# Ten projection steps moved from ahead of the pointwise products to the first attention scores, with counting budgets and four small copies rearranged

## Chip, cores and metric

One core of a Trainium2 chip runs the whole program. The metric is the device time of one execution in microseconds (us), as the median of several runs. The engines are TensorE (PE, matmuls and transposes), VectorE (DVE), ScalarE (ACT) and GpSimd (POOL); SyncE (SP) and ACT issue the transfers (DMA).

## What is computed

A two-layer decoder trunk over 1104 rows: 1040 rows of a prompt (16 learned tokens and 1024 new ones) and 64 rows of eight running sequences. In each layer three mixers work on the same normalised input, and their gated sum goes through an output projection and is added to the input:

```python
(aq, af, ai, az, b_glu, bz, cq, ck, cv, cqi, cki, cw, cz, gate) = project(h, norm_g, w_in, b_in)
oa, s_new = hgrn_prompt(qa, ka, va, logf)                 # gated linear recurrence
ya = (rmsnorm(oa, gn_g) * silu(az)) @ w_pa
y  = silu(layernorm(depthwise_conv(a * sigmoid(g)) + conv_b))
yb = ((y @ conv_pw) * silu(z)) @ w_pb                     # the pointwise products: y @ conv_pw
sc = index_scores(qi, wi, ki)                             # indexer: every query scores every key
idx, valid = select_keys(sc, causal, 256)                 # the 256 best keys of each query
yc = (sparse_attend(rope(q), rope(k), v, idx) * silu(cz)) @ w_pc
h  = h + (ga * ya + gb * yb + gc * yc) @ w_out
```

## The kernel before

Activations stand with channels on the 128 partitions and rows along the free dimension, in three groups of 384, 384 and 336 columns. Each float32 product is made of three matmuls of a split input (`XH`, `XL`: high part and rest) and a split weight (`wh`, `wl`).

**The stream and its fills.** The 60 blocks of 128 output channels of the input projection, and behind them blocks that start the merge, come from one generator, `stream` (L346). A block is 24 steps: three groups of eight, a step is three matmuls. When a group is complete, ACT moves it out of the bank with its bias (`act_`, recorded as L206). Blocks of cz are moved out twice, as they are and through a sigmoid, and POOL multiplies the two (L408); after the third group the block is stored (L411, DMA `czD<-sp`). These tiles come from a pool of two buffers (`spl`, L170). At a block's first step the weights of the block after it are fetched: one load on SP's queue, two ACT copies (`wh`, L271) and two POOL differences (`wl`, L272). PE's order is the order of the program: `fill(key)` puts `FILL[key]` steps of the stream where it is called. In layer 0, added up from the table, the fill "c0" begins at step 1084 of the stream, the fill "aq" ends at step 1246, and the blocks of cz begin at steps 1152, 1176, 1200 and 1224.

**Counting.** The 256 best keys are found by DVE: it counts, bit by bit, how many scores lie over a threshold (L1009), and then builds seven masks, for 1104 columns and then 384 to 1024, from a comparison, an equality, a scan, a second comparison and a combination each (`topk_masks`, L1020). DVE's order is the program's here too; `masks(key)` puts operations there until their nominal ns, columns + 200, use up `SIDE[key]`, and carries the rest as a debt.

**The stretch of the change.** `conv_out` (L1662) runs, in each layer: DVE's difference for the first group, the fill "c0", `masks("c0")`, and then for each of the three groups four products of twelve matmuls on PE (`dense1`, in three banks, `tp`), each multiplied by DVE with the gate (L1693) and stored, with `masks("cc")` behind each; then the next group's difference (L1676), whose gate POOL multiplies (L1678), `masks("c1")` and the fill "c1". `rope_q` (L727) then rotates the queries: loads of R and X, three DVE operations, and stores. `attention` (L1044) loads keys (`kr`) and values (`vr`), transposes the keys on PE (L1063), splits them on ACT and DVE (L1067 to L1070), loads the queries of the last 128 rows, splits them (`Q`, L1088), runs the fill "aq" and makes the first scores (L1107). In these parts ACT, POOL and SP run an order that a planner makes, not the order of the text.

**The tail queries** are part of the indexer: ACT copies four heads of 16 queries into `qt8` (L857), DVE subtracts the copy from the source (L858). DVE's order holds the convolution's 31 taps between (L1594).

Of the kernel before, what the change touches and what calls it, by code (L numbers as in the profile page):

```python
# [11 lines left out]
def _quiet(msg, *args, **kwargs):  # L12
# [33 lines left out]

FILL = {"n0": 10, "n1": 3, "n2": 0, "s0": 7, "s1": 0, "s2": 3, "ic": 35, "ik": (0, 3, 7), "iq": 7, "is": (6, 4, 7, 6, 7, 7),
# [4 lines left out]
SIDE = {"t0": (5000, 10000, 10000, 10000, 9300, 10000), "tr": (2400, 2400, 2400, 2400, 2400, 2400, 2400, 600, 0),  # L52
# [3 lines left out]
KSEL = 4  # L56
KEEP = 24
EDGE = {mybir.EngineType.DVE, mybir.EngineType.Activation}
# [98 lines left out]
def trunk(tc, a, o, depth=DEPTH):  # L157
# [4 lines left out]
    def f(x):  # L162
        return x.bitcast(F32)
# [41 lines left out]
    def act_(out, in_, fn, **kw):  # L205
        S.activation(out, in_, fn, **kw)  # L206
# [76 lines left out]
    def dense1(w, K, xh, xl, nn, slot=None, between=()):  # L283
        wh, wl = w
        ps = (slot or mmt)()
        ops = [(wh(k), x(k)) for k in range(K) for x in (xh, xl)] + [(wl(k), xh(k)) for k in range(K)]
        between = iter(between)
        for n, (wk, x) in enumerate(ops):
            T.matmul(ps[:, 0:nn], wk, x, start=(n == 0), stop=(n == 3 * K - 1))  # L289
            if n % 6 == 5:  # L290
                next(between, None)
        return ps[:, 0:nn]

    def cols_of(t, n0, nn, k0=0):
        return lambda k: t[:, k0 + k, n0:n0 + nn]
# [140 lines left out]
    class Counting:  # L436
# [23 lines left out]
        def rest(self):  # L460
            while self.high is not None:
                self.ahead()
# [136 lines left out]
    def layer(l, hst, late):  # L599
# [46 lines left out]
        SC8 = scp.tile([128, NT], F32, name="SC8", tag="SC8")  # L646
        fill("ic")
        indexer(l, CTr, SC, SC8, fill, taps, act)
        ctr.close()
        tk1 = tks.enter_context(tc.tile_pool(name="tk1", bufs=1))  # L650
# [19 lines left out]
        with tc.tile_pool(name="tk2", bufs=1) as tk2:  # L670
            masks = Side(itertools.chain(side.gen, topk_masks(SC, SC8, MB, MB8, F, tk2)))
            conv_out(l, pv, pw, late_groups, fill, masks)
            rope_q()
            masks.flush()
# [84 lines left out]
    def indexer(l, CTr, SC, SC8, fill, taps, act):  # L759
        with tc.tile_pool(name="ixc", bufs=1) as xc, tc.tile_pool(name="ixt", bufs=2) as xt:  # L760
# [63 lines left out]
            for i in range(7, 1, -1):  # L824
# [3 lines left out]
                for h in range(4):  # L828
                    ps = lgt()
                    for c0 in range(0, n, 512):  # L830
                        c1 = min(n, c0 + 512)
# [23 lines left out]
            for h in range(4):  # L855
                j, e = divmod(h, 2)
                S.copy(qt8[0:64, h, :], (lo8 if e == 0 else hi8)[:, j, 0:16])  # L857
                V.tensor_tensor(qt8[64:128, h, :], (lo8 if e == 0 else hi8)[:, j, 0:16], f(qt8[0:64, h, :]), op=OP.subtract)  # L858
            CH = ((0, 512), (512, 1024), (1024, NT))

# [15 lines left out]
            for g in range(2):  # L876
                ps = lgt()
                for b in (0, 2):
# [9 lines left out]
                    for n in range(2):  # L888
                        for e in range(2):
                            r, c0 = slice(64 * e, 64 * e + 64), 512 * (n ^ e)  # L890
# [771 lines left out]
    def conv_out(l, pv, pw, groups, fill, masks):  # L1662

        with tc.tile_pool(name="cv2", bufs=2) as c2:
            def load(g):
                n0, nn = groups[g]
                sl = slice(n0, n0 + nn)
                yg, bz, BH, BL = (c2.tile([128, 4, 384], dt, name=nm, tag=nm, bufs=bf)[:, :, 0:nn]
                                  for nm, dt, bf in (("yg", F32, 1), ("bzt", F32, 2), ("BH", F32R, 2), ("BL", F32R, 1)))
                Y.dma_start(yg, yD[:, :, sl].rearrange("c p n -> p c n"))  # L1670
                Y.dma_start(bz, fD["bz"][:, :, sl].rearrange("c p n -> p c n"))
                for c in range(4):
                    S.copy(BH[:, c], yg[:, c])

                def rest():
                    V.tensor_tensor(BL, yg, f(BH), op=OP.subtract)  # L1676
                    act_(yg, bz, AF.Sigmoid)
                    G.tensor_tensor(bz, bz, yg, op=OP.mult)  # L1678
                    return bz, BH, BL

                return rest

            nxt = load(0)()
            fill.upto(32)
            fill("c0")
            masks("c0")
            for g, (n0, nn) in enumerate(groups):
                bz, BH, BL = nxt
                if g < 2:
                    rest = load(g + 1)  # L1690
                for c in range(4):
                    ps = dense1(pw[c], 4, cols_of(BH, 0, nn), cols_of(BL, 0, nn), nn, tpt)
                    V.tensor_tensor(bz[:, c], ps, bz[:, c], op=OP.mult)  # L1693
                    Y.dma_start(obD[c, :, n0:n0 + nn], bz[:, c])
                    masks("cc")
                if g < 2:
                    nxt = rest()
                masks("c1")
                fill("c1", g)


# [173 lines left out]
```

## Time and profile before

| | us |
|---|---|
| median of 3 runs | 2865.78 |
| lowest and highest | 2864.01, 2873.34 |
| the profiled execution, its own time | 2876.56 |
| its span, first to last instruction | 2874.7 |
| PE busy in the span | 2741.0 (95%) |
| DVE, ACT, POOL busy | 2022.6, 1357.9, 1252.4 |
| mean granted clock of PE | 0.985 |

An engine's busy time is an average over stages with different limits. Times in the rows count from the span's first instruction. A wait is put down to what ended last before it. A granted clock of 1.00 is 2.4 GHz, of 0.50 1.2 GHz.

### The profile page before, as it was taken

How to read it: one execution, taken by the hardware profiler on the slowest of the kernel's cores; microseconds unless marked ns; L12 is line 12 of the kernel's file. 1: busy time of each engine (PE TensorE's matmuls, PEld its weight loads, DVE VectorE, ACT ScalarE, POOL GpSimd, SP SyncE). 2: the span in 40 equal slices, each digit the busy share in tenths (PEclk: the TensorE clock that was granted, in tenths of full speed). 3: DMA queues.
4: the chain of work that ended last, by engine and by line, in shares of the span. 5: the costliest groups of instructions: out<-in, count | busy, mean ns of one | idle time of the engine just before them, and what ended most of it. 6: DMA issues, size and time to landing. Idle time of an engine off the chain costs nothing. (4 is left out here: it accounts for less than half of the span.)

```text
span 2874.7 us, 45280 instructions
## 1 busy us (share of the span) xinstructions
PE 2741.0 (95%) x17094; PEld 2607.7 (91%) x17094; DVE 2022.6 (70%) x3518; ACT 1357.9 (47%) x2913; POOL 1252.4 (44%) x1012
## 2 busy tenths in 40 slices
PE   7999989999998999999999999999999989999898
PEld 7999878999998998879999997899999989988798
DVE  5789966878986667545258699688888866774543
ACT  4324546773333556544342345577533245665432
POOL 3544344434424115756464352444444331168453
PEclk9999999999999999999999999999999999999999
DMA  4423233332344224665553232413331442257554
GB/s 149 158 83 113 91 123 121 120 120 98 107 155 150 76 68 151 211 199 175 161 166 108 81 102 99 166 68 117 130 131 62 160 152 76 84 157 234 180 155 151
DMA packets 192570, 374.16 MB, mean 130 GB/s; under 512 B 30656, under 2 KB 129696, under 8 KB 192288
## 3 DMA queue, kind: packets, MB, share of 16 engines
q1 hardware_dynamic: 161856, 270.11, 29.9%
q10 hardware_dynamic: 24608, 80.19, 7.1%
q0 software_dynamic: 5888, 20.97, 2.3%
q8 instruction: 134, 2.20, 0.3%
q14 instruction: 84, 0.69, 0.1%
HBM read 251.07 MB, written 122.40 MB: 130 GB/s over the span
## 5 line engine op out<-in xcount | busy, mean ns | idle before, releaser
L396 PE MATMUL mm<-xh,wh 128*128 128x384 f32 (+2 forms) x2656 | 889.5, 337 | 36.5 <-ACT sp L206 33.0
L396 PE MATMUL mm<-xl,wh 128*128 128x384 f32 (+2 forms) x2656 | 884.9, 336 | 0.0
L272 POOL TENSOR_TENSOR wl<-wr,wh 128x512 fp32r<-128x512 f32 x332 | 483.9, 1474 | 748.4 <-ACT wh L271 468.2
L396 PEld LDWEIGHTS mm<-xh,wh 128*128 128x128 f32 x2656 | 506.3, 191 | 50.8 <-ACT sp L206 40.2
L396 PE MATMUL mm<-xh,wl 128*128 128x384 f32 (+2 forms) x2656 | 525.3, 333 | 0.0
L396 PEld LDWEIGHTS mm<-xl,wh 128*128 128x128 f32 x2656 | 506.3, 191 | 6.9 <-issue 1.4
L396 PEld LDWEIGHTS mm<-xh,wl 128*128 128x128 f32 x2656 | 455.3, 190 | 6.2 <-issue 1.4
L206 ACT ACTIVATE sp<-mm,vec 128x384 f32<-128x384 f32 (+1 forms) x356 | 198.4, 564 | 386.4 <-PE mm L396 371.4
L1009 DVE TENSOR_SCALAR_CACHE_REDUCE jk<-SC,F 128x1024 uint8<-128x1024 f32 (+6 forms) x320 | 334.2, 1044 | 7.8
L1594 DVE SCALAR_TENSOR_TENSOR cy<-up,vec,cy 128x1040 f32<-128x1040 f32 x240 | 336.9, 1404 | 0.5
L271 ACT CAST wh<-wr 128x512 fp32r<-128x512 f32 x352 | 204.3, 617 | 116.3 <-PE mm L396 42.1
L206 ACT ACTIVATE P<-P,nm 128x896 f32<-128x896 f32 (+7 forms) x128 | 99.5, 778 | 72.8 <-DVE nm L1114 70.9
L1130 DVE TENSOR_TENSOR pl<-tp,ph 128x512 fp32r<-128x512 f32 x144 | 97.6, 686 | 36.1 <-ACT ph L1129 35.3
L1595 DVE SCALAR_TENSOR_TENSOR cy<-us,vec,cy 128x64 f32<-128x64 f32 x240 | 118.4, 493 | 0.0
L206 ACT ACTIVATE ja<-SC,hB,hz 80x1104 int8<-80x1104 int16 (+1 forms) x120 | 111.4, 929 | 0.2 <-issue 0.2
L1129 ACT CAST ph<-tp 128x512 fp32r<-128x512 f32 x144 | 83.2, 584 | 54.6 <-PE tp L1126 50.1
L1114 DVE CUSTOM_DVE_ANT_0 P<-sc,MB 128x512 f32<-128x512 f32 (+1 forms) x96 | 63.9, 667 | 55.2 <-PE sc L1108 54.2
L1118 DVE TENSOR_SCALAR P<-P,nm 128x896 f32<-128x896 f32 (+7 forms) x128 | 88.9, 695 | 4.2
L1126 PE MATMUL tp<-ident,P 128*128 128x128 f32 x576 | 87.5, 274 | 1.5 <-DVE P L1118 1.5
L206 ACT ACTIVATE rl<-lg 128x1024 f32<-128x1024 f32 (+6 forms) x54 | 42.6, 789 | 88.9 <-DVE SC L842 35.6
L1107 PE MATMUL sc<-KD,Q 128*128 128x512 f32 (+2 forms) x208 | 71.0, 344 | 11.8 <-DVE Q L1088 7.9
L289 PE MATMUL tp<-xh,wh 128*128 128x384 f32 (+2 forms) x240 | 80.3, 337 | 0.4 <-DVE z L1780 0.4
(472 smaller groups left out, 6072.5 us busy)
## 6 DMA issues: line engine op xcount, KB each, us to landing
wr<-in_wp SPq DMA_DIRECT2D x180, 512.0 KB
eg<-gateD SPq DMA_DIRECT2D x80, 184.0 KB
gateD<-sp ACTq DMA_DIRECT2D x24, 552.0 KB
gateD<-sp ACTq DMA_DIRECT2D x24, 544.0 KB
cr<-in_wc SPq DMA_DIRECT2D x16, 290.0 KB
gt<-gateD SPq DMA_DIRECT2D x24, 192.0 KB
za<-zaD SPq DMA_DIRECT2D x24, 192.0 KB
ggD<-sp ACTq DMA_DIRECT2D x8, 552.0 KB
```

The lines of the kernel that those rows point to most:

```text
L206: S.activation(out, in_, fn, **kw)
L271: S.copy(wh[:, k:k + 4], wr[:, k:k + 4])
L272: (eng or G).tensor_tensor(wl[:, k:k + 4], wr[:, k:k + 4], f(wh[:, k:k + 4]), op=OP.subtract)
L289: T.matmul(ps[:, 0:nn], wk, x, start=(n == 0), stop=(n == 3 * K - 1))
L396: T.matmul(ps, w, x, start=(j == 0), stop=(j == 23))
L1009: V.tensor_scalar(jk[0:rows, 0:n], s, F.bitcast(F32)[0:rows, j:j + 1], None, op0=OP.is_ge, op1=OP.add, accum_out=cnt[0:rows, j:j + 1])
L1118: V.tensor_scalar(p[:, 0:n], p[:, 0:n], nm[:, 3:4], None, op0=OP.mult)
L1126: T.transpose(ps[:, 128 * c:128 * c + 128], P[c][:, 128 * kt:128 * kt + 128], ident)
L1129: S.copy(ph, ps)
L1130: V.tensor_tensor(pl, ps, f(ph), op=OP.subtract)
L1594: V.scalar_tensor_tensor(yp, up[:, j:j + 1040], w, yp, op0=OP.mult, op1=OP.add)
L1595: V.scalar_tensor_tensor(ys, us[:, :, j:j + 8], w, ys, op0=OP.mult, op1=OP.add)
```

## The change

The fill "c0" takes 49 steps instead of 59 and the fill "aq" 26 instead of 16. The counting budget ahead of the first product is 14000 instead of 12000, behind each product 1500 instead of 1200, and behind the three groups 2500, 4500 and 6000 instead of 6000 each. The four copies of the tail queries are written ahead of the four differences.

```diff
-        "hl": (5, 6, 5, 5, 9, 6, 16), "hk": 2, "hs": (0, 1, 0, 1, 0, 1, 0, 4), "ho": 2, "ht": 10, "c0": 59,
-        "c1": (13, 22, 52), "aq": 16, "av": (2, 2, 2, 2, 2, 1, 3, 2), "a0": 6, "as": (3, 1, 1, 1, 2, 1, 0, 1),
+        "hl": (5, 6, 5, 5, 9, 6, 16), "hk": 2, "hs": (0, 1, 0, 1, 0, 1, 0, 4), "ho": 2, "ht": 10, "c0": 49,
+        "c1": (13, 22, 52), "aq": 26, "av": (2, 2, 2, 2, 2, 1, 3, 2), "a0": 6, "as": (3, 1, 1, 1, 2, 1, 0, 1),
...
-        "hs": 1000, "hk": 4000, "ho": 500, "ht": 2000, "he": 5500, "c0": 12000, "cc": 1200, "c1": 6000}
+        "hs": 1000, "hk": 4000, "ho": 500, "ht": 2000, "he": 5500, "c0": 14000, "cc": 1500, "c1": (2500, 4500, 6000)}
...
             for h in range(4):
                 j, e = divmod(h, 2)
                 S.copy(qt8[0:64, h, :], (lo8 if e == 0 else hi8)[:, j, 0:16])
+            for h in range(4):
+                j, e = divmod(h, 2)
                 V.tensor_tensor(qt8[64:128, h, :], (lo8 if e == 0 else hi8)[:, j, 0:16], f(qt8[0:64, h, :]), op=OP.subtract)
...
-                masks("c1")
+                masks("c1", g)
                 fill("c1", g)
```

## Rows read from the trace of the kernel before

**Rows 1.** Waits of PE, 800 to 935 us: us in total, times, longest.

```profile
PE sc L1107 <- DVE Q L1088: 3.9, 1, 3.9
PE tp L289 <- DVE bzt L1693: 2.6, 1, 2.6
PE mm L396 <- ACT sp L206: 2.2, 2, 1.9
PE tp L1063 <- DMA kr<-kvD: 1.2, 1, 1.2
```

**Rows 2.** The same waits of PE over the whole span, both layers.

```profile
PE sc L1107 <- DVE Q L1088: 7.9, 2, 3.9
...
PE tp L289 <- DVE bzt L1693: 5.6, 2, 3.0
```

**Rows 3.** Timeline of DVE, layer 0: start, us, operation, in brackets idle before.

```profile
839.29 0.78 DVE L1034 TENSOR_SCALAR eq<-SC,F 80x1104 bf16<-80x1104 f32 x1
...
842.36 0.56 DVE L1693 TENSOR_TENSOR bzt<-tp,bzt 128x384 f32<-128x384 f32 x1 [2.28 <-PE tp L289]
...
842.83 2.44 DVE L1036 TENSOR_TENSOR_SCAN cs<-eq 80x1104 f32<-80x1104 bf16 x1
...
845.64 1.35 DVE L1038 SCALAR_TENSOR_TENSOR eq<-cs,need,eq 80x1104 bf16<-80x1104 f32 x1
...
889.28 0.50 DVE L1693 TENSOR_TENSOR bzt<-tp,bzt 128x336 f32<-128x336 f32 x1
...
902.83 1.31 DVE L740 TENSOR_TENSOR R<-R,C 128x1104 f32<-128x1104 f32 x1 [6.84 <-DMA X<-rD]
```

**Rows 4.** The timeline of PE, layer 0, from the products to the transposes.

```profile
840.01 0.33 PE L289 MATMUL tp<-BH,ph 128*128 128x384 f32 x1
...
886.12 0.33 PE L396 MATMUL mm<-xh,wh 128*128 128x384 f32 x1
...
907.61 0.42 PE L396 MATMUL mm<-xh,wh 128*128 128x336 f32 x1 [1.88 <-ACT sp L206]
...
907.87 0.32 PE L396 MATMUL mm<-xl,wh 128*128 128x336 f32 x1
...
915.96 1.06 PE L1063 MATMUL tp<-ident,kr 128*128 128x128 f32 x8 [1.25 <-DMA kr<-kvD]
```

**Rows 5.** The timeline of ACT with its DMA issues, layer 0.

```profile
910.14 0.38 ACTq L1056 DMA_DIRECT2D kr<-kvD  x1
...
915.14 0.34 ACTq L411 DMA_DIRECT2D czD<-sp  x1
...
921.99 0.58 ACT L206 ACTIVATE sp<-mm,vec 128x384 f32<-128x384 f32 x1 [1.87 <-DMA czD<-sp]
...
922.60 0.58 ACT L1067 CAST KD<-tp 64x512 fp32r<-64x512 f32 x1
```

**Rows 6.** Windows: stretch, length, busy time by engine, granted clock, DMA share, GB/s.

```profile
809.30:840.00 30.70, 30.70 (x179) 30.22 (x178) 25.79 (x54) 10.83 (x20) 9.27 (x5) 1.00 0.67 225
...
864.90:868.30 3.40, 3.40 (x13) 3.39 (x12) 3.36 (x5) 0.00 (x0) 0.00 (x0) 0.51 0.26 90
...
930.20:933.40 3.20, 3.20 (x12) 2.92 (x11) 1.52 (x5) 1.03 (x1) 0.04 (x1) 0.53 0.32 84
```

**Rows 7.** The timeline of DVE, layer 0, two operations drawn out.

```profile
855.85 2.75 DVE L1034 TENSOR_SCALAR eq<-SC,F 128x512 bf16<-128x512 f32 x1
...
880.93 1.58 DVE L1034 TENSOR_SCALAR eq<-SC,F 128x896 bf16<-128x896 f32 x1
```

**Rows 8.** The timeline of POOL, the product beside the first of them.

```profile
854.50 3.83 POOL L1678 TENSOR_TENSOR bzt<-bzt,yg 128x1536 f32<-128x1536 f32 x1
```

**Rows 9.** The timeline of ACT, layer 0, at the tail queries' copies.

```profile
315.01 0.17 ACT L857 CAST qt<-tp 64x16 fp32r<-64x16 f32 x1 [5.87 <-DVE qt L858]
```

**Rows 10.** The timeline of PE behind those copies, layers 0 and 1.

```profile
316.65 0.42 PE L396 MATMUL mm<-xh,wh 128*128 128x336 f32 x1 [1.23 <-ACT sp L206]
...
1739.10 0.43 PE L396 MATMUL mm<-xh,wh 128*128 128x336 f32 x1 [1.23 <-ACT sp L206]
```

## The prediction

> **What bounds the kernel now.** I read the list of waits of TensorE (PE) first, in the stretch that the change touches: from the pointwise products to the attention's first scores, 800 to 935 us in layer 0. PE waits 9.9 us there, of which 3.9 for the scaled queries Q, 2.6 for a pointwise product's VectorE (DVE) step, 2.2 for ScalarE (ACT) and 1.2 for the keys kr [rows 1]; the list over the whole span adds layer 1, with the same Q wait and a product wait of 3.0 [rows 2]. PE runs an order written out by hand, so all PE work before the first scores plus all its waits gives the time of the first scores; what matters is which chain ends last there.
>
> Then DVE's timeline. DVE counts until 840.07, sits idle 2.28 us, multiplies the first product at 842.36, and from then on is never idle until the last product (889.28 + 0.50) [rows 3]. From that product a chain of transfers runs through the rotation of the queries (X lands for 902.83 [rows 3]) to kr, whose landing frees PE at 915.96 [rows 4]; ACT issues the load of kr at 910.14, after the rotation [rows 3, 5]. I infer that kr's tile lies in memory that the rotation gives back, and take kr to follow the last product at a fixed 26.2 us. Layer 1 I take to repeat all this, as its two waits do [rows 2]. From kr to the first scores at 929.60 (925.68 + 3.92) [rows 1, 4], ACT and DVE split keys and queries, and ACT stands 1.87 us behind the store of a gated block (czD) ahead of the third key copy [rows 5].
>
> **The change part by part.**
>
> *Ten steps leave the fill ahead of the products.* The 59 steps there take 30.70 us [rows 6], 0.52 each, so the products begin 5.2 us earlier, at 834.8 instead of 840.01 [rows 4]. The same ten come back in the fill behind the key transposes, so PE's work before the first scores is unchanged; only its waits can change. With the stream as counted from the fill table, the products begin at step 1133 instead of 1143. The weights of the second cz block (a load on SP's queue, two ACT copies, two GpSimd differences) move from the first fill between products to the second, those of the third block from the second to the last, those of the block after the four from the last fill to behind the query load. The last is the only one that passes a queue's urgent work: its load stands behind the query load, and its copies have at least the 10 steps that were brought there (5.2 us) as cover; without it each us of delay would be a PE wait.
>
> *Counting is spread.* I count the debts by hand. The budget of 14000 adds two operations ahead of the first product, the scan of 2.44 us and the comparison of 1.35 [rows 3]; the later budgets give them back. Up to the last product exactly the same operations stand before as after. So DVE comes to the first product at 840.07 + 2.4 + 1.3 = 843.8. PE has three banks for products: it does three by 834.8 + 6.3 = 841.1 and then waits for DVE to free one at 844.3. **That is a new wait of 3.2 us**, larger than the 2.6 that it had at the second group [rows 1]. In exchange DVE's idle 2.28 us is gone. A wait that long costs more: after the 2.6 us wait the granted clock was 0.51 (the 1.2 GHz level) for 3.4 us [rows 6], which is 1.65 us of PE time. It moves from the second group to the first, where the products that follow wait for DVE anyway.
>
> DVE thus reaches the last product 2.3 us earlier, plus or minus its collisions. An eq of 512 columns took 2.75 us, where one of 1104 columns took 0.78 [rows 3, 7]; it ended 0.3 us after GpSimd's product of 3.83 us [rows 7, 8]. Six operations are drawn out so, from that eq to the eq of 896 columns that took 1.58 [rows 7]; against their pace by columns elsewhere they lose about 8.3 us together, and I put 0.3 less after: 2.6 earlier, bounds 0 and 5. The Trainium skill ("SBUF — State Buffer", Who interferes with whom) says that a two-input DVE operation and a GpSimd operation exclude each other for a whole instruction. By that rule the second group's first product cannot begin before the GpSimd product that follows its difference, near 859.4; if they overlapped it would begin near 856. The trace agrees with the rule, which speaks against moving counting out of the stretches without such products.
>
> *Arrival at kr.* kr lands at 915.96 - 2.6 = 913.4; I take 913.5, because the first cz block's store now meets the rotation's loads. PE leaves the last product at about 882.6 (886.1 before [rows 4]), and 52 steps with a store wait of 1.9 as before (907.61 [rows 4]) bring it to 911 to 912. It waits some 1.5 us for kr; that wait is the slack that hides a store wait of up to 1.4 us at the preceding block boundary, which the dense products hid before.
>
> *From kr to the scores.* Before: 929.60 - 3.92 - 915.96 = 9.7, less a 0.3 wait for ACT, is 9.4 us of PE work. After it is 9.4 + 5.2 = 14.6. Now a boundary between two cz blocks lies four steps into this fill instead of six steps before the transposes. The next block's first evacuation needs the finished block's store. Before, the store issued at 915.14 released ACT at 921.99, 6.85 us later [rows 5]. After: transposes 1.1 [rows 4], four steps, evacuation, GpSimd product and store put the release at 925 to 928.5, while PE runs out of banks at 913.5 + 1.1 + 20 x 0.52 = 925.0. **Wait 0 to 3; I take 1.6**, the middle, since both the store's time and ACT's order are open. First scores: 913.5 + 14.6 + 1.6 = 929.7, against 929.60: +0.1. Q would be ready by 927.1 if its chain kept its 13.6 us, so its 3.9 us wait goes and PE's own work is what comes last.
>
> What is gained is the clock. After the 3.92 us wait the clock was 0.53 from 930.2 to 933.4 with PE busy throughout [rows 6], again 1.65 us. A wait of 1.6 leaves it up (the 1.88 at 907.61 was followed by a matmul of 0.32 us, the usual length [rows 4]). So -1.65.
>
> *The tail queries' copies.* Now ACT's second copy waits 5.87 us for the first difference on DVE, which stands behind convolution taps [rows 9]; behind it on ACT stand evacuations, and PE waits 1.23 us for one in each layer [rows 10]. With all four copies first, ACT never waits for DVE here. The three copies (0.17 each [rows 9]) now delay one earlier evacuation by about 0.4 us, which PE feels in layer 0. Worth 0.8 to 1.2 per layer; bounds 0 and 1.3, taken 0.9.
>
> **Sum.** +0.1 - 1.65 - 0.9 = -2.4 per layer, -4.8 in both. The profiled execution took 2876.56 us (span 2874.7), above the three timed runs and 10.8 over their median of 2865.78. The difference is applied to both: 2871.8 in a profile like it, 2861.0 as a median.
>
> **The rivals.**
> *The wait only moves (no change).* The store wait in the last fill reaches 2.8 instead of 1.6 and the clock falls there: +1.2 and +1.65 per layer against -2.4, about 0, so 2866. For it: the store took 6.85 us [rows 5] and ACT has key copies to do at that moment. Against: the DMA queues are emptier once kr and vr have landed.
> *DVE collides less (faster).* The last product comes 5 us earlier, kr at 911; PE is then limited by its own fill, arrives at 911.5, and with a store wait of 0.5 scores start at 926.6: -3.0 - 1.65 - 0.9 = -5.5 per layer, 2854.8. For it: 8.3 us of collisions are there to be avoided. Against: GpSimd's products follow the same differences in both orders.
> *ACT's queue holds the key copies (slower).* ACT takes the first evacuation behind the store ahead of the third key copy, as it does now at 921.99 and 922.60 [rows 5]. Now this costs 1.87 us; after it the store would release ACT at 927.1, the copy would start at 927.7, and the 7.0 us that separate copy and first scores now (922.60 to 929.60) give 934.7: +5.1 per layer, the clock falls as before, with -0.9 for the copies +4.2, in all +8.4: 2874.2. It decides when the evacuation stands ahead of that copy. Against: the block's first group is now ready 4.2 us later, well after the copy's own inputs.
> *The copies do not do what is said.* If something else holds them, the 0.9 falls away: 2862.8, inside the forecast's own range.
>
> **How the numbers follow.** Forecast 0.50 (own range 2857 to 2864), no change 0.23, faster 0.17, slower 0.10. The faster and the slower case are each cut at about half, leaving 0.16 outside 2854 to 2871. A measurement of this kernel can tell some 0.3%, 8.6 us, from no change, so faster means under 2857.2 (the faster case and the forecast's edge: 0.21), slower over 2874.4 (half of the slower case and a little: 0.06), same 0.73.
>
> **What would show it.** Right: no DVE idle ahead of the first product; a PE wait near 3.2 us at the first group's fourth product with the clock at half behind it, and none over 1 us at the second group; kr 2 to 3 us earlier, counted from the end of DVE's first counting; no wait for Q, and the clock at 1.00 over the first scores; ACT's four tail copies in a row and no 1.23 us wait of PE behind them. Wrong: a Q wait that stays, a store wait over 2.6 us in the last fill, or a last product less than 1 us earlier.

## The result and the profile after

| | before | after |
|---|---|---|
| median of 4 runs each, us | 2866.25 | 2895.57 |
| lowest and highest, us | 2864.01, 2873.34 | 2888.44, 2896.82 |
| the profiled execution, its span, us | 2876.56, 2874.7 | 2888.44, 2886.5 |
| mean granted clock of PE | 0.985 | 0.986 |
| first difference to first scores, layer 0, us | 107.25 | 120.02 |
| the same, layer 1, us | 106.03 | 121.15 |

The ratio is 1.0081, with a 95% interval of 1.0063 to 1.0099: 18 to 28 us slower, where 5 us faster was forecast. The last two lines of the table measure the stretch of the change, from DVE's difference for the first group of products to PE's first scores (822.35 to 929.60 us before, 814.74 to 934.76 after). It grew by 12.8 and 15.1 us, together 27.9 of the 29.3 us between the two medians. Outside the two stretches the profiled execution took 2661 us before and 2645 after, and between 2642 and 2665 in the kernels run below, so the stretch, and not the span, is compared.

PE's waits after the change, 800 to 960 us (us in total, times, longest), to be held against [rows 1]:

```profile
PE mm L396 <- ACT sp L206: 14.8, 4, 8.0
PE tp L289 <- DVE bzt L1695: 2.9, 1, 2.9
PE sc L1109 <- DVE Q L1090: 2.2, 1, 2.2
...
```

The same in layer 1, 2235 to 2380 us:

```profile
PE mm L396 <- ACT sp L206: 15.9, 4, 8.4
PE tp L289 <- DVE bzt L1695: 3.4, 1, 3.4
...
```

One line has grown, PE's wait for a bank that ACT has not moved out: 2.2 us before, 14.8 after. (Behind line 857 the line numbers of after are two higher: L1693 became L1695.) PE's timeline of after shows where; the number in brackets is the idle time before the instruction. It answers to [rows 4]:

```profile
836.88 0.45 PE L289 MATMUL tp<-BH,ph 128*128 128x384 f32 x1 [2.94 <-DVE bzt L1695]
...
863.80 0.44 PE L396 MATMUL mm<-xh,wh 128*128 128x384 f32 x1 [2.44 <-ACT sp L206]
...
878.08 1.40 PE L396 MATMUL mm<-xh,wl 128*128 128x336 f32 x8
...
895.85 0.65 PE L396 MATMUL mm<-xh,wh 128*128 128x336 f32 x1 [7.98 <-ACT sp L206]
...
914.00 0.43 PE L396 MATMUL mm<-xh,wh 128*128 128x336 f32 x1 [3.64 <-ACT sp L206]
...
917.30 1.24 PE L1065 MATMUL tp<-ident,kr 128*128 128x128 f32 x8
...
929.53 0.42 PE L396 MATMUL mm<-xh,wh 128*128 128x336 f32 x1 [0.76 <-ACT sp L206]
...
934.76 0.79 PE L1109 MATMUL sc<-KD,Q 128*128 128x512 f32 x1 [2.17 <-DVE Q L1090]
```

The block that ends at 879.5 (878.08 + 1.40) is the one whose end counts. PE still finds free banks for the next block until 895.85 - 7.98 = 887.87, then stands still for 8 us. The transposes at 917.30 wait for nothing: kr was there before PE was. Now ACT, with its DMA issues, behind that end:

```profile
879.52 0.97 ACT L206 ACTIVATE sp<-mm,vec 128x336 f32<-128x336 f32 x2
886.18 0.33 ACTq L411 DMA_DIRECT2D czD<-sp  x1
886.61 0.58 ACT L206 ACTIVATE sp<-mm,vec 128x384 f32<-128x384 f32 x1 [6.11 <-POOL sp L408]
895.22 1.52 ACT L206 ACTIVATE sp<-mm,vec 128x384 f32<-128x384 f32 x3 [8.03 <-DMA czD<-sp]
...
905.54 0.33 ACTq L411 DMA_DIRECT2D czD<-sp  x1
906.13 0.38 ACTq L1058 DMA_DIRECT2D kr<-kvD  x1
```

A cz block uses both buffers of its pool, one for its values and one for their sigmoid. The next block's first evacuation takes the one that POOL's product gives back (886.61), its second the one that the store gives back (895.22). From the end of the block's last evacuation (880.49) it is 5.7 us to the store's issue and 9.0 from there to its landing. POOL in the same time:

```profile
879.72 4.57 POOL L272 TENSOR_TENSOR wl<-wr,wh 128x512 fp32r<-128x512 f32 x2 [9.26 <-DMA obD<-bzt]
884.25 1.89 POOL L408 TENSOR_TENSOR sp<-sp 128x336 f32<-128x336 f32 x1
...
902.10 2.54 POOL L272 TENSOR_TENSOR wl<-wr,wh 128x512 fp32r<-128x512 f32 x2 [4.20 <-ACT wh L271]
```

and SP's queue, whose loads for the rotation are issued just ahead of the store:

```profile
878.68 1.27 SPq L328 DMA_DIRECT2D eg<-gateD  x3
...
881.52 1.76 SPq L739 DMA_DIRECT2D X<-rD  x2
...
895.33 0.33 SPq L743 DMA_DIRECT2D rD<-R  x1
904.66 0.33 SPq L269 DMA_DIRECT2D wr<-in_wp  x1
905.04 1.31 SPq L745 DMA_DIRECT2D qD<-rD  x2
```

The kernel before has a boundary whose store bares its price too, the second one, and it has the same boundary as above, covered. These are ACT's rows there, of before, first the covered one and then the bare one:

```profile
877.79 0.97 ACT L206 ACTIVATE sp<-mm,vec 128x336 f32<-128x336 f32 x2
883.32 0.33 ACTq L411 DMA_DIRECT2D czD<-sp  x1
889.50 1.05 ACT L206 ACTIVATE sp<-mm,vec 128x384 f32<-128x384 f32 x2 [10.75 <-PE mm L396]
...
897.38 0.97 ACT L206 ACTIVATE sp<-mm,vec 128x336 f32<-128x336 f32 x2
900.91 0.33 ACTq L411 DMA_DIRECT2D czD<-sp  x1
901.63 0.58 ACT L206 ACTIVATE sp<-mm,vec 128x384 f32<-128x384 f32 x1 [3.28 <-PE mm L396]
906.98 1.52 ACT L206 ACTIVATE sp<-mm,vec 128x384 f32<-128x384 f32 x3 [4.77 <-DMA czD<-sp]
```

and of POOL at the bare one:

```profile
897.47 2.55 POOL L272 TENSOR_TENSOR wl<-wr,wh 128x512 fp32r<-128x512 f32 x2 [0.61 <-ACT wh L271]
899.98 0.90 POOL L408 TENSOR_TENSOR sp<-sp 128x336 f32<-128x336 f32 x1
```

Bare, it took 2.6 us from the evacuation's end (898.35) to the issue and 6.1 to the landing, 8.6 in all, and PE waited 1.88 [rows 4]. After the change the first boundary takes 5.7 + 9.0 = 14.7, which is 6.1 more, and 1.88 + 6.1 = 8.0 is the wait measured. Half of the 6.1 is POOL, which delays the store's issue (4.57 + 1.89 against 2.55 + 0.90), and half is the store itself (9.0 against 6.1). Covered, the same boundary of before cost nothing, though POOL was late there too (the issue at 883.32, 4.6 us behind 878.76): PE was busy with the third group's products until 886.12 [rows 4], and ACT waited for PE and not for the store when it came to the next block (889.50, 10.75 <-PE).

Last DVE and the clock. DVE's first and last product, and its first rotation step, to be held against [rows 3]:

```profile
836.27 0.55 DVE L1695 TENSOR_TENSOR bzt<-tp,bzt 128x384 f32<-128x384 f32 x1
...
877.42 0.51 DVE L1695 TENSOR_TENSOR bzt<-tp,bzt 128x336 f32<-128x336 f32 x1
...
891.10 1.31 DVE L740 TENSOR_TENSOR R<-R,C 128x1104 f32<-128x1104 f32 x1 [5.72 <-DMA X<-rD]
```

and windows behind four of PE's waits (columns as in [rows 6], the granted clock is the 1.00 and the 0.50 ahead of the DMA share):

```profile
836.50:840.00 3.50, 3.12 (x18) 3.13 (x19) 3.47 (x9) 0.00 (x0) 0.00 (x0) 1.00 0.34 114
...
895.80:899.20 3.40, 3.35 (x12) 3.35 (x13) 0.00 (x0) 0.94 (x3) 1.97 (x2) 0.50 0.41 166
913.90:917.00 3.10, 3.00 (x11) 3.00 (x12) 0.00 (x0) 0.99 (x3) 1.99 (x2) 0.56 0.63 183
...
934.70:938.00 3.30, 3.24 (x9) 2.86 (x10) 2.15 (x6) 1.57 (x2) 0.00 (x0) 0.51 0.32 79
```

So the 12.8 us of layer 0 are: 10.0 us more waits of PE (14.8 + 2.9 + 2.2 = 19.9 against 9.9 [rows 1]), and 1.4 more lost to the clock inside the stretch (3.4 x 0.50 + 3.1 x 0.44 = 3.1 against 3.4 x 0.49 = 1.7 [rows 6]). The remaining 1.4 is not placed.

### The profile page after: what moved, and what is told of

It is laid out like the page before. It is cut to its first block, busy times and chain, and to the rows that moved or that the text cites. A ratio compares the mean times of both kernels' runs of the same rounds, so it can differ in the third digit from the quotient of the medians.

```text
span 2886.5 us, 45283 instructions
## 1 busy us (share of the span) xinstructions
PE 2739.9 (95%) x17094; PEld 2606.2 (90%) x17094; DVE 2018.9 (70%) x3518; ACT 1358.3 (47%) x2913; POOL 1244.9 (43%) x1012
## 5 line engine op out<-in xcount | busy, mean ns | idle before, releaser
L396 PEld LDWEIGHTS mm<-xh,wh 128*128 128x128 f32 x2656 | 508.1, 191 | 76.9 <-ACT sp L206 66.9
L1596 DVE SCALAR_TENSOR_TENSOR cy<-up,vec,cy 128x1040 f32<-128x1040 f32 x240 | 331.1, 1380 | 0.5
L1597 DVE SCALAR_TENSOR_TENSOR cy<-us,vec,cy 128x64 f32<-128x64 f32 x240 | 124.3, 518 | 0.0
```

Source lines behind the costliest of these rows:

```text
L396: T.matmul(ps, w, x, start=(j == 0), stop=(j == 23))
L1596: V.scalar_tensor_tensor(yp, up[:, j:j + 1040], w, yp, op0=OP.mult, op1=OP.add)
L1597: V.scalar_tensor_tensor(ys, us[:, :, j:j + 8], w, ys, op0=OP.mult, op1=OP.add)
```

## The experiments

The theory: the ten steps were what stood between the end of a cz block and the need for its buffer; moved, the blocks end earlier among PE's other work, the dense products no longer cover POOL's product and the store, and PE waits for them. Rivals: the counting delays DVE and with it everything; kr, Q or the rotation's transfers are late by themselves; POOL and not the store is late.

Ratios are to runs of the kernel before on the same chip; the stretch is that of the table above.

| what is run | median us | ratio, 95% | stretch, layers 0 and 1 |
|---|---|---|---|
| copies alone | 2869.09 | 1.0006, 0.9994 to 1.0018 | 106.4, 106.2 |
| counting alone | 2866.90 | 0.9990, 0.9980 to 1.0000 | 106.0, 104.6 |
| ten steps alone | 2890.23 | 1.0082, 1.0063 to 1.0100 | 118.4, 117.8 |
| ten steps back at once | 2867.43 | 0.9990, 0.9979 to 1.0000 | 106.5, 107.0 |
| ten steps to behind the last product | 2888.76 | 1.0068, 1.0049 to 1.0086 | 116.8, 117.6 |
| ten steps from there to the scores | 2875.92 | 1.0025, 1.0015 to 1.0034 | 110.7, 110.7 |
| after, store by groups | 2876.96 | 1.0032, 1.0017 to 1.0048 | 113.5, 115.0 |
| before, store by groups | 2868.33 | 0.9992, 0.9982 to 1.0002 | 107.0, 106.6 |
| after, store from another tile | 2871.57 | 1.0011, 0.9998 to 1.0025 | 107.9, 110.2 |
| before, counting later | 2859.57 | 0.9969, 0.9957 to 0.9981 | 104.2, 102.6 |
| the same, store by groups | 2857.89 | 0.9959, 0.9946 to 0.9972 | 102.6, 102.5 |
| before, counting later still | 2882.96 | 1.0048, 1.0035 to 1.0061 | 115.6, 114.4 |

**The three parts, one by one.** The copies alone:

```diff
             for h in range(4):
                 S.copy(qt8[0:64, h, :], ...)
+            for h in range(4):
                 V.tensor_tensor(qt8[64:128, h, :], ...)
```

> Only the four tail copies ahead of the four differences; fills and counting budgets as before. Theory 1 (the store of a cz block holds its two buffers, and the ten moved steps put block boundaries where no products cover it): nothing of the loss, so 1 to 6 us under the kernel before, ACT's 5.9 us wait and PE's 1.2 us wait behind it gone in both layers. Theory 2 (the spread counting costs): the same. Theory 3 (the new place of the copies changes what the planner does with ACT, POOL and SP everywhere behind it): most of the 29 us is here, so 2885 or more.

Nothing that can be measured, in either direction. ACT's wait ahead of the copies and PE's 1.23 us behind them [rows 10] are gone, as expected, but an evacuation that now stands behind all four copies makes PE wait earlier:

```profile
309.09 0.45 PE L396 MATMUL mm<-xh,wh 128*128 128x384 f32 x1 [1.71 <-ACT sp L206]
```

At this place it was 0.58 us before. In all PE's waits here are 1.7 us against 1.8 before in layer 0, and 1.7 against 1.2 in layer 1 (1.74 at 1728.53); in after they are 0.9 and 1.7.

The counting alone:

```diff
-"c0": 12000, "cc": 1200, "c1": 6000
+"c0": 14000, "cc": 1500, "c1": (2500, 4500, 6000)
```

> Only the counting budgets changed; steps and copies as before. Theory 1: the products start as late as before and DVE merely has two operations more ahead of them, so 0 to 4 us either way. Theory 2: 15 us or more over the kernel before. Theory 3: about as before.

The wait for a product's step is gone in layer 0 and 0.9 us in layer 1, but the store wait at the second boundary is 4.0 and 2.7 us (ACT 4.3 and 3.5 in all, against 2.2 and 1.7 before), and Q's 3.9 us has not moved: a small preview of what follows. No gain beyond the edge of what can be told.

The ten steps alone:

```diff
-"c0": 59, ... "aq": 16
+"c0": 49, ... "aq": 26
```

> Only the ten steps moved from the fill ahead of the products to the fill behind the key transposes; budgets and copies as before. Theory 1: the whole loss, 20 to 32 us over the kernel before, and PE's waits for ACT between products and first scores near 15 us a layer as in the changed kernel (2.2 before). Theory 2: under 8 us over the kernel before, because DVE's order is that of before. Theory 3: about as before.

The whole loss: 1.0082 beside 1.0081. PE's waits of layer 0 in this kernel:

```profile
PE mm L396 <- ACT sp L206: 13.3, 4, 8.0
...
```

The counting, so, is no cause of the loss, and the copies are none.

**Which place of the ten steps.** After, with the ten steps given back in the fill behind the first group of products:

```diff
-"c1": (13, 22, 52), "aq": 26
+"c1": (23, 22, 52), "aq": 16
```

> The changed kernel, but the ten steps come back in the first fill between the products (23 steps instead of 13) and the fill behind the key transposes has 16 again, so that the boundaries of the cz blocks stand where they stood against the second and third group of products and against the scores; counting and copies as in the change. Theory 1: the loss is gone, between 12 us under and 4 us over the kernel before, PE's waits for ACT in the stretch back to 2 to 4 us a layer. Theory 2: the loss stays, 15 us or more over the kernel before.

The loss is gone, though the products still begin ten steps earlier; ACT's waits are 0.4 and 2.5 us. It is the stretch between the second group and the scores that lacks the steps. Before, with the ten steps taken from ahead of the products to behind the last one:

```diff
-"c0": 59, "c1": (13, 22, 52)
+"c0": 49, "c1": (13, 22, 62)
```

> The kernel before, but the ten steps come back in the last fill between products and key transposes (62 steps instead of 52), not behind the transposes. So the two earlier block boundaries (into the first cz block and from the first to the second) lie uncovered as in the changed kernel, while the boundary from the third to the fourth lies where it was before. If the loss is at the earlier boundaries: first difference to first scores 115 to 120 us a layer (107 and 106 before, 118 with the ten steps moved behind the transposes), 16 to 28 us in all. If it is at the boundary behind the transposes: 106 to 109 a layer, under 6 us in all.

Nearly all of the loss is there (1.0068), with the fill ahead of the scores as it was. ACT at the first boundary of this kernel:

```profile
890.91 0.33 ACTq L411 DMA_DIRECT2D czD<-sp  x1
...
899.55 1.52 ACT L206 ACTIVATE sp<-mm,vec 128x384 f32<-128x384 f32 x3 [7.63 <-DMA czD<-sp]
```

It is the same picture as after: the issue late by POOL, 8.6 us to the landing, PE idle 7.9 us. So the boundary in the last fill, on which the prediction spent most of its care, is not the place. And the other half of the move by itself, from behind the last product to ahead of the scores:

```diff
-"c1": (13, 22, 52), "aq": 16
+"c1": (13, 22, 42), "aq": 26
```

> The kernel before, with ten steps taken from the last fill between products and key transposes (42 instead of 52) to the fill behind the transposes (26 instead of 16). Only the boundary from the third to the fourth cz block moves, from six steps ahead of the transposes to four steps behind them. If the loss is at the earlier boundaries: 104 to 109 us a layer, between 6 us under and 5 over the kernel before. If it is at this boundary, as the prediction's slower rival had it: 112 or more a layer, 10 us or more in all.

It costs a quarter per cent, by another wait; the 110.7 us lie between the two cases that were expected. Here the boundaries stay covered (ACT 0.9 and 0.2 us) and PE, ten steps short of work ahead of the transposes, waits for the keys and values:

```profile
PE tp L1063 <- DMA vr<-kvD: 6.5, 1, 6.5
```

**The store or POOL.** First the store cut in three, each group of a cz block stored as soon as it is gated, in after and in before:

```diff
-                    if g == 2:
+                    if nm == "cz":
+                        S.dma_start(fD[nm][c, :, sl], bufs[i][:, sl])
+                    elif g == 2:
```

> The changed kernel, but each cz block is stored group by group as its groups are done, so that only a third of it is still to be stored at the block's end. If the length of the store (9.0 us from issue to the release of ACT at the first boundary) holds PE: the wait of 8 falls to 2 to 4, first difference to first scores 108 to 114 a layer, 12 us or more under the changed kernel. If the late issue holds it (GpSimd multiplies the last group only behind the weights' differences, 5.7 us after ACT is done with the block): 117 or more, within 6 us of the changed kernel.

> The kernel before with the cz blocks stored group by group. Its waits for ACT in the stretch (2.2 and 1.7 us) should be gone, but the wait for Q ends last there, so most of that goes into the Q wait: 0 to 3 us under the kernel before, first difference to first scores 104 to 107. If it is 4 us or more faster, the store also held the key copies on ACT.

In after it gives back some 60% of the loss in time and about half of it in the stretches, but the large wait stays, 7.4 of 8.0 us (5.4 of 8.4 in layer 1). So neither case came as it was written: the time is nearer to the first, the wait in layer 0 to the second. ACT in that kernel:

```profile
890.53 0.33 ACTq L410 DMA_DIRECT2D czD<-sp  x1
...
898.34 0.58 ACT L206 ACTIVATE sp<-mm,vec 128x384 f32<-128x384 f32 x1 [6.79 <-DMA czD<-sp]
```

The last third, 336 of 1104 columns, takes 7.8 us to land where the whole block took 9.0: at this place the time is mostly not the store's size. The second boundary does gain (at 912.69 ACT waits 3.13 us, against 6.17 in after). In before the cut changes nothing, as the covered boundaries let one expect.

Then the wait itself taken away, by a store of equal size that reads another tile, so that no buffer waits for it (the gated values do not reach memory, so only the times count):

```diff
-S.dma_start(fD[nm][c, :, lo:NT], bufs[i][:, lo:NT])
+S.dma_start(fD[nm][c, :, lo:NT], f(XH[:, c, lo:NT]) if nm == "cz" else bufs[i][:, lo:NT])
```

> The kernel after the change, except that the store of a cz block reads another tile (the projections' input, which nothing overwrites here) instead of the block's own tile. Its size, its place on ACT's queue and all steps stay; the block's tile is only no longer held until the store has landed. Left out: the gated values do not reach the memory that the attention reads, so the times alone are to be read. Theory (TensorE waits at the block boundaries because the finished block's tile is held by its store until that lands): ScalarE's 8.0, 2.4 and 3.6 us waits of TensorE between products and first scores go down to 1 us or less each, the stretch from the first difference of the products to the first scores falls from 120.0 and 121.2 us to 105 to 110, and the time from 2895 to 2858 to 2872. Rival (GpSimd is late with the block's gate products, 4.57 us for a pair in place of 2.54, and the next block's evacuations wait for that): the waits stay at 5 us or more, the stretch at 115 or more, and the time at 2885 or more. Rival (the keys' landing is what comes last, and the boundaries only fill the time up to it): the waits on ScalarE go and as many us of wait appear at the key transposes; the stretch at 113 to 118.

The store did not keep its place on ACT's queue, though that was expected. Its new source is ready long before, and layer 0's four stores were issued between 54.73 and 60.99 us, layer 1's between 1454.51 and 1460.03:

```profile
60.99 0.35 ACTq L411 DMA_DIRECT2D czD<-xh  x1
```

So this kernel has no cz store in the stretch at all, neither one that holds a buffer nor its transfer and its issue on ACT's queue, and the run does not tell these apart. PE's waits of layer 0 in this kernel:

```profile
...
PE mm L396 <- ACT sp L206: 2.5, 3, 1.5
PE tp L1065 <- DMA vr<-kvD: 2.3, 1, 2.3
...
```

ACT's share falls from 14.8 to 2.5 us, the stretch by 12.2 and 11.0 us, the time to 0.11% above before (-0.02 to 0.25%). POOL's pair was late here too (5.33 us at 883.85) and ACT waited for its product, but PE waited only 0.17 us for that (892.18): without a store, POOL's lateness costs next to nothing. The largest of the three waits, 1.46 us at 905.97, stands behind the issue of kr's load on ACT's queue (904.38). In layer 1 a wait of 6.8 us for the rotation's write-back (`qD<-rD`) has come up in place of part of it, which is why that layer gains less: with the store away, the transfers behind the rotation are next.

How POOL and the store share the wait, the other kernels' boundaries show. Take the time from the end of ACT's last evacuation of a block to the landing of its store, the two parts added up above. Of the kernels that store a block whole in this stretch (ten, with before and after), 26 first and second boundaries made PE wait, and at each the wait is that time less 6.74 to 6.76 us in layer 0 and less 6.59 to 6.60 in layer 1. The part up to the issue, POOL's, ranges over them from 2.6 to 6.1 us, and the store's from 2.7 to 9.4. In the kernel with the counting alone the second boundary has 2.9 + 7.8 us and a wait of 3.98; in the next kernel below, where POOL alone is late, 5.5 + 4.3 and a wait of 3.08. So the theory holds, and POOL is no rival of it but one of its two parts: each us by which POOL delays the store's issue, or by which the store lands later, is a us of PE's wait once the boundary is uncovered. The transfers to the keys are what is next in line.

**A version faster than both.** Since the end of the products starts the rotation and DVE stands idle ahead of the rotation's data (6.84 us [rows 3]), counting can stand there instead of between the products:

```diff
-"c0": 12000, "cc": 1200, "c1": 6000
+"c0": 13000, "cc": 900, "c1": (4500, 4500, 20000)
```

> The kernel before, with the counting alone moved: less of it ahead of the first product and between the products' groups (budgets 13000, 900, and 4500 twice), and what is left over put behind the last product (20000), where VectorE has idle time ahead of the rotation. Theory (the last product's time on VectorE sets the rotation, the rotation sets the keys' landing, and the block boundaries stay covered as in the kernel before): the last product comes some 5 to 6 us earlier, the 2.6 us wait for a product's step goes, the stretch from the first difference to the first scores falls from 107.3 and 106.0 us to 100 to 104, and the time by 6 to 11 us, to 2855 to 2860. Rival (what does not change with the products is late next: a cz block's store, as in the kernel after the change): the last product earlier by as much, but ScalarE's waits of TensorE grow by 4 us or more per layer and the stretch stays at 105 to 108, the time within 4 us of 2866. Rival (the counting behind the last product delays the rotation's own steps on VectorE): the stretch 107 or more, the time 2866 to 2874.

0.31% faster than before. The last product comes 61.0 us behind the first difference instead of 66.9, and the rotation starts with no idle time ahead of it. DVE in this kernel:

```profile
896.52 2.01 DVE L740 TENSOR_TENSOR R<-R,C 128x1104 f32<-128x1104 f32 x1
```

and PE's waits in layer 0:

```profile
...
PE mm L396 <- ACT sp L206: 3.1, 1, 3.1
...
```

and ACT at the second boundary:

```profile
897.40 0.33 ACTq L411 DMA_DIRECT2D czD<-sp  x1
...
901.72 0.58 ACT L206 ACTIVATE sp<-mm,vec 128x384 f32<-128x384 f32 x1 [3.31 <-DMA czD<-sp]
```

Q's wait of 3.9 us is as before. The rival has a small part: PE's wait for ACT is 3.1 us against 2.2 before, since POOL's pair (4.51 us at 891.01) now stands beside DVE's counting and the store is issued 5.5 us behind the last evacuation (891.88) instead of 2.6. The gain of 3.0 and 3.4 us per layer is nearer to what the rotation's first step gained, counted from the first difference (3.7 and 2.5 us), than to what the last product gained (6.0 and 6.6). The last loads for the rotation were issued by 886.6; in before, after and the kernel with the move in the last fill alone its first step stands 6.6 to 7.8 us behind that (5.4 in the kernel without a cz store beside them), so here it could have begun 2 to 3 us sooner than at 896.52, and little is left to be filled. With the store cut in three besides:

> The kernel with the later counting, and besides each group of a cz block stored by itself as soon as it is gated. Theory (in the kernel with the later counting the rotation, the keys and Q end last, 3.9 us of wait for Q; the 3.1 us store wait lies ahead of the keys' landing and is filled by it): the store wait goes or halves, what it frees comes back as a wait at the key transposes or for Q, the stretch stays at 102 to 104.5 us and the time at 2856 to 2862. Rival (the store wait is on the path as well): the stretch falls by 3 us per layer, and the time to 2851 to 2855. Rival (the extra stores delay the rotation's loads, which now come 8 us earlier than in the kernel before): the stretch grows by 1 to 3 us, 2861 to 2866.

The store wait falls to 1.8 in layer 0 and is 3.9 in layer 1, Q's is 3.4; 0.41% faster than before, and the two intervals overlap, so the cut's own gain is not told apart from none. And with still more of the counting behind the last product:

```diff
+"c0": 11000, "cc": 600, "c1": (3000, 3000, 30000)
```

> The kernel before, with still more of the counting behind the last product (budgets 11000, 600, 3000 twice, the rest behind). Theory (VectorE has about 7 us between the last product and the rotation's data, which the kernel with the later counting already uses up: its rotation began with VectorE busy until then): the last product comes 3 to 6 us earlier again, the rotation does not, since VectorE counts until about 896; the stretch stays within 1.5 us of 104.2 and 102.6, the time at 2857 to 2863. Rival (the last product alone sets the rotation): 3 to 6 us per layer less, 2847 to 2855. Rival (the counting now delays the rotation by more than the products gain): the stretch 105 or more, 2862 to 2870.

Slower, by the third case and by far more than its figure. The counting was expected to end at about 896 us; it ended at 907.6. The last loads for the rotation were issued by 884.7; by the same 6.6 to 7.8 us, its first step came some 15 us late. PE's wait and DVE's row:

```profile
PE tp L1063 <- DMA kv<-kvD: 15.5, 1, 15.5
```

```profile
907.63 1.99 DVE L740 TENSOR_TENSOR R<-R,C 128x1104 f32<-128x1104 f32 x1
```

The last product gained only 1 us more (59.9 behind the first difference), since DVE now waited for PE among the products (3.02 us ahead of one of them). DVE's idle time ahead of the rotation has a size, and past it each operation of counting delays the keys.

## Why the prediction was wrong, point by point

**Right.** The first product came 12.7 us behind the first difference instead of 17.7, 5.0 earlier where 5.2 was worked out. The new wait at the first group's fourth product was put at 3.2 us and was 2.94 (3.4 in layer 1). The idle 2.28 us of DVE ahead of its first product is gone (836.27). The last product came 4.2 us earlier, counted from the first difference (62.7 us against 66.9), and 3.4 in layer 1; 2.6 was taken, with bounds of 0 and 5.

**The step that failed: the store wait "of up to 1.4 us" that a slack would hide.** The prediction saw that the dense products hid the first boundary between cz blocks before. It kept the second boundary at its 1.9 us and entered nothing for the first, because it would cost at most 1.4 us and a wait for kr would hide that. It did not work the first boundary out from what stands beside it after the change. Measured against the second boundary of before, POOL's pair and product took 3.0 us longer there, beside DVE's counting (the scan and two masks of 1024 columns from 878.68 to 885.4), and the store 3.0 us longer, beside nine loads of SP's queue. At the second boundary of before DVE was idle while POOL worked, and the rotation's loads were about to land (902.83 [rows 3], 1.9 us behind the store's issue). That the loads made the store longer is inferred from this; no run here moves them alone. The term was taken at 0 to 1.4 us and measured 7.98, the second boundary's 1.9 measured 3.64, and the wait for kr that was to be the slack did not come. An unlisted 2.44 us came at 863.80, at the boundary into the first cz block: on ACT a gate's activation (861.99) stands ahead of the evacuation. It overwrites `yg`, which DVE's difference reads, and that difference stands behind the counting on DVE and ended at 861.90 (860.36 + 1.54). The three waits ahead of the transposes (2.44 + 7.98 + 3.64) cost 14.1 us where 1.9 stood in the sum. The third boundary between cz blocks, in the last fill, was put at 1.6 with bounds of 0 and 3, and measured 0.76 (1.44 in layer 1): the one boundary that was worked out from its own surroundings was the one that came out.

**kr at a fixed 26.2 us behind the last product.** This failed too, though it set no time any more. From the last product (877.42 + 0.51) to the transposes it was 39.4 us. The rotation's data were ready at the usual distance (R at 891.10, 13.7 us behind the product's start, as 902.83 is behind 889.28), but `rD` was written at 895.33 and the write-back `qD` came only at 905.04: SP's queue held a weight load (904.66) between them, that load waited for POOL's differences (902.10 + 2.54), these for ACT's copies, and those for the block that the store had held up. The issue of kr (906.13) stood behind the second block's store (905.54) on ACT's queue. A fixed distance between two events holds only as long as nothing on the queues between them waits for something else.

**Q's wait.** It was said to go; 2.17 us are left. Q's halves on ACT (933.37) stand behind the copies of the next block's weights (932.32), which waited 1.90 us for PE itself, so Q is tied to PE's last steps ahead of the scores. The third boundary's store is not what holds it: in the kernel whose store reads another tile there is no such store, and Q's wait is the same 2.17 us. The clock over the first scores, which was to stay at 1.00, is 0.51. Of the 1.65 us that this was to bring, nothing came (and 3.2 us at 0.53 [rows 6] are 1.5 us rather than 1.65).

**The copies.** 0.9 us per layer was taken: 1.23 us of PE's wait gone, less about 0.4 for an earlier evacuation that the copies delay. The 1.23 went, but PE's wait for the earlier evacuation grew by more: with the copies alone by 1.1 us in layer 0 (1.71 for 0.58) and 1.7 in layer 1, in after by 0.3 and 1.7. So PE's waits changed by -0.1 and +0.5 us there, by -0.9 and +0.4 in after, and the copies alone gave a ratio of 1.0006 (0.9994 to 1.0018). How much of the growth is the copies' own is not shown.

**GpSimd's product in the second group.** The prediction put the second group's first product near 859.4, 37.0 us behind the first difference, and it came at 36.5 (851.25 - 814.74). That does not bear out the exclusion that it was drawn from: the product reads the tile that GpSimd's product writes, so it has to wait for it either way. What does speak for one is a mask of 512 columns that started beside that product and took 3.87 us on DVE (847.46), where before it took 0.69.

**The rivals.** None held. The slower one had the right kind of thing, ACT's queue behind a store, but at the boundary in the last fill, and for 5 us per layer instead of 13 and 15. What was missing is a rival that sums all boundaries, each with its own surroundings.

## What to carry to other kernels

When work is moved in a hand-written order, every periodic boundary of the shifted stream (a block's end, its store, the next weights) lands beside other work: price each boundary where it lands, from what DVE, POOL and the queues do there, and ask what covered it before. A covered wait has no row in the list of waits, and its price isn't that of the bare one next to it. To gain from idle time on one engine, fill it only as far as its rows show it idle: with 15 us of counting behind the last product instead of 6 the kernel was 0.3% faster, with 29 us it was 0.5% slower than before.

## What was not expected of the hardware

The store of a third of a block took 7.8 us to land, a whole one 9.0, a whole one 6.1 at another place, and in the kernel with the counting later still a whole one took 2.7 (issued at 895.28, landed by 898.02): its size did not set its time. That the other transfers in flight did is likely, but no run shows it by itself.

The length of a wait did not tell whether PE's clock fell. After 2.94 us (836.88) the granted clock was 1.00, and after 2.17 us (934.76) it was 0.51; before the change 2.6 us were enough for 0.51 [rows 6]. The prediction charged 1.65 us for the first of these, which was not lost.

POOL's pair of differences took 2.54 us at 902.10, with DVE idle, and 4.57 at 879.72, beside DVE's counting. The Trainium skill ("SBUF — State Buffer", Who interferes with whom) says that a DVE instruction with two inputs in SBUF contends with a GpSimd instruction that reads SBUF; these rows agree. In the prediction the rule was used for DVE's loss alone; POOL's, by which the store came late, was left out of the sum.
